# Row-wise dot products with a softmax: one transfer for the first x block, and the last store in two halves on two queues

## The chip, the cores and the metric

The kernel runs on one core of a Trainium2 chip. The metric is the device time of one execution in microseconds (us); before the change it is 320.69 us, the median of three runs (320.68 to 320.96).

## What is computed

```python
B, N, D = 8, 4096, 512          # x, y: float32, B x N x D
gram = np.matmul(x, y.transpose(0, 2, 1))
diag = np.diagonal(gram, axis1=1, axis2=2)
exp = np.exp(diag - diag.max(axis=-1, keepdims=True))
out = exp / exp.sum(axis=-1, keepdims=True)
```

Only the diagonal of the product is used. So the kernel needs, for each of the 8 x 4096 pairs of rows, the dot product of x's row with y's row (512 elements each), and then a softmax over the 4096 results of each batch. Both inputs are read once: 2 x 67.1 MB. The output is 8 x 4096 float32, 0.13 MB.

## The kernel before

**Tiling.** Four batches are worked on at a time (s = 0 and 1). A batch's 4096 rows lie over 32 partitions (G = 32), 128 rows to a partition, so four batches fill 128 partitions. A partition's 128 rows are taken in blocks of R = 32 rows, which makes S = 8 passes, t = 0 to 7: passes 0 to 3 are the first four batches, 4 to 7 the other four. A block is 64 KB in each partition, contiguous in memory, and 8 MB in all for x and the same for y.

**Buffers.** There are two tiles for x (xs, used in turn by t % 2) and a single one for y (ys), and a small tile, side, for the last K = 6 rows of y. The dot products go to diag[s], the softmax to res[s].

**Passes 0 to 5** (L118 to L131). x and y are loaded (load_x L63, load_y L66, both on the SyncE queue, SP). ScalarE copies y's last 6 rows to side (L123). VectorE multiplies the first 26 rows with y in place in xs (products, L70), which frees ys for the next load, then the last 6 with side, and adds up 30 rows (sums, L73). ScalarE adds up the other 2 (sums_act, L78). In pass 0, x comes in two transfers: rows 0 and 1, then rows 2 to 31 (L119 to L121). No instruction uses the first 2 rows alone: the first product reads rows 0 to 25.

**Pass 6** (L133 to L139) loads y in two halves. **Pass 7** (L141 to L150) loads x and y in pieces of 16, 8, 4, 2, 1 and 1 rows (x in pieces of at least 2), each followed by VectorE instructions that multiply and add up one row at a time (dots, L83).

**The end.** The softmax of the first four batches is stored by four transfers of 32 partitions each on SP (L155, L156). They are issued during pass 7. For the second four, exps takes the maximum (L97, L91) and exponentials with their sum (ScalarE, L104), normalize the total, its reciprocal and the product (L91, L110, L111), and ScalarE's queue (ACT) stores res[1], 128 partitions, in one transfer (L158). After it stand only the waits and barriers that end the program (L184 in the profile).

**What sets the order.** The order on each engine is the order in which the lines stand here; nothing is moved by a scheduler. Waits between engines are semaphores that the framework places. Transfers take eight semaphores in turn, so a transfer also waits until the one eight places before it has landed. SP's instructions are almost only such waits and issues: x of pass t+2 waits for the sums of pass t (its tile must be free), y of pass t+1 waits for the products of pass t.

Of the kernel before, what the change touches and what calls it, by code (L numbers as in the profile page):

```python
# [1 line left out]

# [5 lines left out]


@with_exitstack
def kernel(
    ctx: ExitStack,
    tc: tile.TileContext,
    x: bass.AP,
    y: bass.AP,
    out: bass.AP,
):
    nc = tc.nc
    ctx.enter_context(tc.manual_schedule())  # L20
    f32 = mybir.dt.float32
    Alu = mybir.AluOpType
    Act = mybir.ActivationFunctionType
    X = mybir.AxisListType.X
    B, N, D = x.shape
    P = nc.NUM_PARTITIONS
    G = 32
    Q = P // G
    C = N // G
    R = 32  # L30
    H = R // 2
    K = 6
    W = 2
    S = B // Q * (C // R)


    xv = x.rearrange("(s b) (j c) d -> s (b j) c d", b=Q, j=G)
    yv = y.rearrange("(s b) (j c) d -> s (b j) c d", b=Q, j=G)
    ov = out.rearrange("(s b) (j c) -> s (b j) c", b=Q, j=G)

    big = ctx.enter_context(tc.tile_pool(name="big", bufs=1))
    small = ctx.enter_context(tc.tile_pool(name="small", bufs=1))


    xs = [big.tile([P, R, D], f32, name=f"xs{i}") for i in range(2)]
    ys = big.tile([P, R, D], f32, name="ys")
    side = big.tile([P, K, D], f32, name="side")

    diag = [small.tile([P, C + i], f32, name=f"diag{i}") for i in range(B // Q)]
    res = [small.tile([P, C], f32, name=f"res{i}") for i in range(B // Q)]  # L50

    def columns(t, r0, n):
        c0 = t % (C // R) * R + r0
        return slice(c0, c0 + n)

    def rows(t, r0, n):
        return xs[t % 2][:, r0 : r0 + n, :]

    def dots_of(t, r0, n):
        return diag[t * R // C][:, columns(t, r0, n)]  # L60

    def load_x(t, r0, n):
        nc.sync.dma_start(out=rows(t, r0, n), in_=xv[t * R // C, :, columns(t, r0, n), :])  # L63

    def load_y(t, r0, n):
        nc.sync.dma_start(out=ys[:, r0 : r0 + n, :], in_=yv[t * R // C, :, columns(t, r0, n), :])  # L66

    def products(t, r0, n, yt):
        xt = rows(t, r0, n)
        nc.vector.tensor_tensor(out=xt, in0=xt, in1=yt, op=Alu.mult)  # L70

    def sums(t, r0, n):
        nc.vector.tensor_reduce(out=dots_of(t, r0, n), in_=rows(t, r0, n), axis=X, op=Alu.add)  # L73

    def sums_act(t, r0, n):
        for r in range(r0, r0 + n):
            row = xs[t % 2][:, r, :]
            nc.scalar.activation(out=row, in_=row, func=Act.Copy, accum_out=dots_of(t, r, 1))  # L78

    def dots(t, r0, n):  # L80
        for r in range(r0, r0 + n):
            xt = xs[t % 2][:, r, :]
            nc.vector.scalar_tensor_tensor(  # L83
                out=xt, in0=xt, scalar=1.0, in1=ys[:, r, :], op0=Alu.mult, op1=Alu.mult,
                accum_out=dots_of(t, r, 1),
            )

    def over_quadrant(name, column, op, negate=False):

        got = small.tile([P, 1], f32, name=name)  # L90
        nc.vector.tensor_reduce(  # L91
            out=got, in_=column.to_broadcast([P, G]), axis=X, op=op, negate=negate, apply_transpose=True
        )
        return got

    def largest(out, d):
        nc.vector.tensor_reduce(out=out, in_=d, axis=X, op=Alu.max)  # L97

    def exps(i, d):
        mxp = small.tile([P, 1], f32, name=f"mxp{i}")  # L100
        largest(mxp, d)
        nmx = over_quadrant(f"nmx{i}", mxp, Alu.max, negate=True)
        sump = small.tile([P, 1], f32, name=f"sump{i}")
        nc.scalar.activation(out=res[i], in_=diag[i][:, :C], func=Act.Exp, bias=nmx, scale=1.0, accum_out=sump)  # L104
        return sump

    def normalize(i, sump):
        total = over_quadrant(f"sum{i}", sump, Alu.add)
        rc = small.tile([P, 1], f32, name=f"rc{i}")
        nc.vector.reciprocal(out=rc, in_=total)  # L110
        nc.vector.tensor_single_scalar(out=res[i], in_=res[i], scalar=rc, op=Alu.mult)  # L111

    nc.vector.addr_align(128, offset=0, max_nops=0)
    nc.scalar.addr_align(128, offset=0, max_nops=0)

    for t in range(S - 2):  # L118
        if t == 0:  # L119
            load_x(t, 0, 2)  # L120
        load_x(t, 2 if t == 0 else 0, R - 2 if t == 0 else R)  # L121
        load_y(t, 0, R)
        nc.scalar.activation(out=side, in_=ys[:, R - K :, :], func=Act.Copy)  # L123
        if t == C // R:
            normalize(0, sump)
        products(t, 0, R - K, ys[:, : R - K, :])
        products(t, R - K, K, side)
        sums(t, 0, R - W)
        sums_act(t, R - W, W)
        if t == C // R - 1:  # L130
            sump = exps(0, diag[0])  # L131

    t = S - 2  # L133
    load_x(t, 0, R)
    for r0 in (0, H):
        load_y(t, r0, H)
        products(t, r0, H, ys[:, r0 : r0 + H, :])
    sums(t, R - H // 2, H // 2)
    sums_act(t, 0, R - H // 2)  # L139

    t += 1  # L141
    r0 = 0
    for n in (16, 8, 4, 2, 1, 1):
        if r0 < R - 1:
            load_x(t, r0, max(n, 2))
        load_y(t, r0, n)
        if r0 == R - 2:
            largest(diag[1][:, C:], diag[1][:, : C - 2])
        dots(t, r0, n)
        r0 += n  # L150

    met = small.tile([P, C - R], f32, name="met")
    nc.scalar.activation(out=met, in_=diag[1][:, : C - R], func=Act.Copy)  # L153

    for p, n in ((0, G), (G, G), (2 * G, G), (3 * G, G)):  # L155
        nc.sync.dma_start(out=ov[0, p : p + n, :], in_=res[0][p : p + n, :])  # L156
    normalize(1, exps(1, diag[1][:, C - 2 :]))
    nc.scalar.dma_start(out=ov[1], in_=res[1])  # L158


# [1 line left out]
_INS = ['x', 'y']  # L162
_OUTS = [((8, 4096), 'float32')]


# [23 lines left out]
```

## Time and profile before

| | us |
|---|---|
| median of three runs | 320.69 |
| span of the profiled execution | 318.87 |
| between the two | 1.82 |
| VectorE (DVE) busy | 244.7 (77%) |
| ScalarE (ACT) busy | 42.0 (13%) |
| bytes read / written | 134.22 MB / 0.13 MB |
| mean rate over the span | 421 GB/s |
| DMA queue of SP, share of the 16 DMA engines | 97.8% |
| DMA queue of ACT, share of the 16 DMA engines | 0.1% |

The span runs from the first to the last instruction of the profiled execution; the time of a run also holds what lies around it. All times in the text are counted from the span's start. A transfer is cut into packets, one for each partition here, that 16 DMA engines work through, 8 partitions to an engine. Each engine reports when its part has landed, so a transfer has 16 landing records, and the last of them ends the wait for it. The GB/s of a stretch count a packet where it starts; in a short stretch in which many long packets start the figure goes above the rate of the bytes.

### The profile page before, as it was taken

The numbers are of one execution on the slowest core, as the hardware profiler recorded it, in microseconds if no ns is written. First come the engines' busy times: TensorE is split into PE (matmuls) and PEld (weight loads), VectorE is DVE, ScalarE is ACT, GpSimd is POOL, SyncE is SP. The second block draws the span as 40 slices with busy tenths as digits, with TensorE's granted clock in tenths as the row PEclk, the third lists the DMA queues.
The fourth block names the chain that finished last, engine by engine and source line by source line (L and its number), as shares of the span: only waits on it lengthen the run. The fifth ranks groups of instructions, "written<-read, shape, count | busy, mean of one in ns | idle before, by whom it ended". The sixth has DMA issues, their size and how long they took to land.

```text
span 318.9 us, 304 instructions
## 1 busy us (share of the span) xinstructions
DVE 244.7 (77%) x96; ACT 42.0 (13%) x84; POOL 0.2 (0%) x4
## 2 busy tenths in 40 slices
DVE  0000069995899939999399994999949999996995
ACT  1000030100301003010120103000030100197000
POOL 0000000000000000000000000000000000000000
DMA  8989999999999999999999999999999899999993
GB/s 314 493 378 485 436 395 436 485 395 403 510 403 395 477 444 395 427 493 395 403 510 403 395 460 460 395 419 493 403 395 510 358 444 415 444 423 419 421 413 116
DMA packets 4226, 134.37 MB, mean 421 GB/s; under 512 B 512, under 2 KB 768, under 8 KB 1536
## 3 DMA queue, kind: packets, MB, share of 16 engines
q1 hardware_dynamic: 4080, 134.29, 97.8%
q10 hardware_dynamic: 144, 0.07, 0.1%
q14 instruction: 2, 0.02, 0.0%
HBM read 134.22 MB, written 0.13 MB: 421 GB/s over the span
## 4 chain that ended last, share of the span: by engine, by line
DMA 62%; DVE 35%; issue 2%; SPq 0%; ACT 0%; DVEq 0%
DMA ys<-in_y_dram 62%; DVE xs L70 30%; DVE diag L73 4%; DVE xs L83 0%; SPq L63 0%; DVE res L111 0%; DVE nmx L91 0%; DVE sum L91 0%; ACT res L104 0%; DVE rc L110 0%; DVE mxp L97 0%; DVEq L70 0%; SPq L66 0%; DVEq L83 0%
## 5 line engine op out<-in xcount | busy, mean ns | idle before, releaser
L70 DVE TENSOR_TENSOR xs<-xs,ys 128x13312 f32<-128x13312 f32 (+1 forms) x8 | 101.4, 12690 | 66.5 <-DMA ys<-in_y_dram 66.5
L73 DVE TENSOR_REDUCE diag<-xs 128x30 f32<-128x15360 f32 (+1 forms) x7 | 101.3, 14477 | 0.2
L78 ACT ACTIVATE xs<-xs 128x512 f32<-128x512 f32 x36 | 22.2, 616 | 111.0 <-DVE xs L70 111.0
L123 ACT ACTIVATE side<-ys 128x3072 f32<-128x3072 f32 x6 | 16.6, 2764 | 124.0 <-DMA ys<-in_y_dram 124.0
L83 DVE SCALAR_TENSOR_TENSOR xs<-xs,ys 128x512 f32<-128x512 f32 x32 | 19.9, 686 | 3.3 <-DMA ys<-in_y_dram 3.3
L70 DVE TENSOR_TENSOR xs<-xs,side 128x3072 f32<-128x3072 f32 x6 | 20.1, 3351 | 0.0
L78 ACT ACTIVATION_READ_ACCUMULATOR xs<-xs 128x1 f32 x36 | 6.7, 186 | 0.0
L104 ACT ACTIVATE res<-diag,nmx 128x128 f32<-128x128 f32 x2 | 0.8, 402 | 37.6 <-DVE nmx L91 37.6
L83 DVE DVE_READ_ACCUMULATOR xs<-xs,ys 128x1 f32 x32 | 2.6, 81 | 0.0
L123 ACT ACT_TABLE_LOAD x1 | 1.3, 1283 | 1.2 <-PEq L173 1.2
L91 DVE TRANSPOSE_TENSOR_REDUCE sum<-sump 128x1 f32<-128x32 f32 x2 | 0.4, 212 | 1.2 <-ACT res L104 1.2
L111 DVE TENSOR_SCALAR res<-res,rc 128x128 f32<-128x128 f32 x2 | 0.6, 286 | 0.1
L97 DVE TENSOR_REDUCE mxp<-diag 128x1 f32<-128x128 f32 (+1 forms) x2 | 0.4, 220 | 0.1
L91 DVE TRANSPOSE_TENSOR_REDUCE nmx<-mxp 128x1 f32<-128x32 f32 x2 | 0.4, 212 | 0.1
L110 DVE RECIPROCAL rc<-sum 128x1 f32<-128x1 f32 x2 | 0.3, 164 | 0.1
L104 ACT ACTIVATION_READ_ACCUMULATOR res<-diag,nmx 128x1 f32 x2 | 0.4, 186 | 0.0
L97 DVE TENSOR_REDUCE diag<-diag 128x1 f32<-128x126 f32 x1 | 0.3, 284 | 0.1
L153 ACT ACTIVATE met<-diag 128x96 f32<-128x96 f32 x1 | 0.3, 282 | 0.0
L173 POOL MEMSET const-bfloat16-1.0<- 128x1 bf16 x1 | 0.1, 102 | 0.0
L173 POOL MEMSET const-uint8-127<- 128x1 uint8 x1 | 0.1, 102 | 0.0
L173 POOL MEMSET const-float32-0.0<- 128x1 f32 x1 | 0.1, 99 | 0.2 <-issue 0.2
L173 POOL MEMSET const-float32-1.0<- 128x1 f32 x1 | 0.1, 99 | 0.0
## 6 DMA issues: line engine op xcount, KB each, us to landing
ys<-in_y_dram SPq DMA_DIRECT2D x3, 4096.0 KB, 16.0
xs<-in_x_dram SPq DMA_DIRECT2D x1, 7680.0 KB, 21.8
xs<-in_x_dram SPq DMA_DIRECT2D x1, 4096.0 KB, 14.9
xs<-in_x_dram SPq DMA_DIRECT2D x1, 2048.0 KB, 20.5
ys<-in_y_dram SPq DMA_DIRECT2D x1, 2048.0 KB, 17.2
xs<-in_x_dram SPq DMA_DIRECT2D x3, 512.0 KB, 22.1
xs<-in_x_dram SPq DMA_DIRECT2D x1, 1024.0 KB, 19.3
ys<-in_y_dram SPq DMA_DIRECT2D x1, 1024.0 KB, 21.3
```

The costliest lines, as they stand in the source:

```text
L70: nc.vector.tensor_tensor(out=xt, in0=xt, in1=yt, op=Alu.mult)
L73: nc.vector.tensor_reduce(out=dots_of(t, r0, n), in_=rows(t, r0, n), axis=X, op=Alu.add)
L78: nc.scalar.activation(out=row, in_=row, func=Act.Copy, accum_out=dots_of(t, r, 1))
L83: nc.vector.scalar_tensor_tensor(out=xt, in0=xt, scalar=1.0, in1=ys[:, r, :], op0=Alu.mult, op1=Alu.mult, accum_out=dots_of(t, r, 1),)
L91: nc.vector.tensor_reduce(out=got, in_=column.to_broadcast([P, G]), axis=X, op=op, negate=negate, apply_transpose=True)
L97: nc.vector.tensor_reduce(out=out, in_=d, axis=X, op=Alu.max)
L104: nc.scalar.activation(out=res[i], in_=diag[i][:, :C], func=Act.Exp, bias=nmx, scale=1.0, accum_out=sump)
L110: nc.vector.reciprocal(out=rc, in_=total)
L111: nc.vector.tensor_single_scalar(out=res[i], in_=res[i], scalar=rc, op=Alu.mult)
L123: nc.scalar.activation(out=side, in_=ys[:, R - K :, :], func=Act.Copy)
L153: nc.scalar.activation(out=met, in_=diag[1][:, : C - R], func=Act.Copy)
L173: nc = _bacc.Bacc("TRN2", target_bir_lowering=False, num_devices=1)
```

## The change

In pass 0, x is loaded in one transfer of 32 rows, as in the other passes. The last store is issued as two transfers: partitions 0 to 63 on SP, partitions 64 to 127 on ACT.

```diff
     for t in range(S - 2):
-        if t == 0:
-            load_x(t, 0, 2)
-        load_x(t, 2 if t == 0 else 0, R - 2 if t == 0 else R)
+        load_x(t, 0, R)
         load_y(t, 0, R)
...
     normalize(1, exps(1, diag[1][:, C - 2 :]))
-    nc.scalar.dma_start(out=ov[1], in_=res[1])
+    nc.sync.dma_start(out=ov[1, : 2 * G, :], in_=res[1][: 2 * G, :])
+    nc.scalar.dma_start(out=ov[1, 2 * G :, :], in_=res[1][2 * G :, :])
```

Instructions of VectorE, ScalarE and GpSimd stay as they are and in the same order. SP issues one load less at the start, and one store of 64 partitions more after the four stores of L156.

## The prediction

> **What bounds the kernel now.** I read the table of stretches first, one row for each pass of the loop over t. Its columns are the stretch and its length, busy us and instructions of DVE, ACT and POOL, the granted TensorE clock, the mean share of the 16 DMA engines, GB/s.
>
> ```profile
> 1.50:42.50 41.00, 0.04 (x1) 1.08 (x2) 0.00 (x0) 1.00 1.02 435
> 42.50:81.10 38.60, 33.41 (x3) 3.95 (x5) 0.00 (x0) 1.00 1.00 435
> 81.10:119.80 38.70, 33.45 (x3) 4.10 (x5) 0.00 (x0) 1.00 1.00 434
> 235.90:274.70 38.80, 38.74 (x4) 4.10 (x5) 0.00 (x0) 1.00 0.98 423
> 294.10:313.40 19.30, 18.90 (x61) 0.00 (x0) 0.00 (x0) 1.00 0.99 408
> 313.40:318.90 5.50, 2.34 (x9) 0.49 (x2) 0.00 (x0) 1.00 0.04 13
> ```
>
> The DMA engines are full from the first bytes to 313.4; VectorE has 5 us to spare in a pass. The next view, the chain that ended last in order of time, seems to say "DMA, then VectorE, then DMA", but its VectorE pieces are covered: while VectorE multiplies, x of the next pass streams in. The landing records of the trace (16 for each transfer, one from each DMA engine) settle it. From the last engine's landing of one 8 MB transfer to that of the next there are 19.34 to 19.36 us, from x of pass 1 to x of pass 6, without a longer step; the 4 MB ones take 9.71. So all that lies behind the first transfers hangs on one point: when the slowest DMA engine reaches steady flow. Move that by d, and all moves by d down to the last load (313.94), the 2.4 us of VectorE and ScalarE behind it, and the last store.
>
> **The first step's x.** The chain's beginning, and (second fence) the issues of the first 5 us with their size and time to landing:
>
> ```profile
> 0.73 0.40 SPq L63
> 1.13 0.06 issue
> 1.18 0.42 SPq L63
> 1.60 0.05 issue
> 1.65 40.68 DMA ys<-in_y_dram
> ```
>
> ```profile
> xs<-in_x_dram SPq DMA_DIRECT2D x1, 7680.0 KB, 21.8
> xs<-in_x_dram SPq DMA_DIRECT2D x1, 512.0 KB, 4.1
> ys<-in_y_dram SPq DMA_DIRECT2D x1, 40.7
> ```
>
> The 2 rows (512 KB) land 4.1 us after their issue, at 4.84; the 30 rows at 22.99, y at 42.33. 30 rows therefore cost 18.15 us in steady flow and 32 rows 19.35: **2 rows inside a long transfer cost 1.20**. Two rows as a transfer of their own cost 1.28 near the end (landing to landing, the 2-row x at 310.09 to 311.37 and 311.37 to 312.66). At the start they cost more. Stretches of half a microsecond:
>
> ```profile
> 0.00:1.75 1.75, 0.00 (x0) 0.59 (x1) 0.20 (x4) 1.00 0.00 0
> 1.75:2.25 0.50, 0.00 (x0) 0.50 (x1) 0.00 (x0) 1.00 0.98 229
> 2.25:2.75 0.50, 0.00 (x0) 0.19 (x1) 0.00 (x0) 1.00 0.67 221
> 2.75:3.25 0.50, 0.00 (x0) 0.00 (x0) 0.00 (x0) 1.00 1.14 344
> ```
>
> Until 3.25 the engines deliver 221 to 344 GB/s, against 435. The packet records tell how: the transfer is 128 packets of 4 KB, 8 for each engine. The first starts at 1.756; they last 234 ns in the mean and up to 655, where the 4 KB packets near the end last 163 ns. The first 60 KB packet of the 30 rows starts at 3.55 on the quickest engine, at 3.97 in the mean, at 4.44 on the slowest. From 1.756 that is 1.80 and 2.69 us for 8 packets that cost 1.28 when all runs: 0.5 us lost on the quickest engine, up to 1.4 on the slowest (less its own later start, which the records, without engine names, don't give). The spread of 0.9 us then stays to the end of the run.
>
> After the change the first transfer is 128 packets of 64 KB (the pieces the other full transfers have), and y's issue moves up by one slot of 0.45 us, behind 19 us of x: nothing comes of that. What the slowest engine saves is (4.44 minus its new starting point) minus 1.20. From both sides:
>
> - Least: all that was lost at the start is lost again. Saved are 1.28 - 1.20 = 0.08.
> - Most: it starts at 1.756 and loses nothing: 4.44 - 1.76 - 1.20 = 1.48.
>
> What decides is whether a slow first access hides behind a long packet. The nearest row is y of pass 0: a tensor not touched before, in 64 KB packets, and its 128 packets last 2.42 us in the mean, 2.51 at most, with no delay in its landings. A wait of some 0.3 us for a row's first bytes is seen when the packet ahead lasts 0.16 us, not when it lasts 2.42. So I take 7 of 8 such waits as hidden. Two things stay: the wait of each engine's first packet, 0.1 to 0.4 us by the packets above their 0.16 (165 to 524 ns among the first), and two packets of 8 KB of instructions that start at 1.77 and 2.89 and cost 2 x 0.31 = 0.62 us of some engine, probably the slowest. With them it starts at 1.76 + 0.62 + (0.1 to 0.5) = 2.5 to 2.9, so 4.44 - 1.20 - 2.5 to 2.9 = 0.3 to 0.75 saved. I take **-0.5**.
>
> The cover could go elsewhere: the instruction packets may now wait behind 64 KB packets, 2.4 us each. ScalarE first needs its table at 42.36 and VectorE works from 42.46, so this costs nothing.
>
> **The last store.** Timeline, the page's line on the issue, then two stretches:
>
> ```profile
> 316.16 0.29 DVE L111 TENSOR_SCALAR res<-res,rc 128x128 f32<-128x128 f32 x1
> 316.48 0.38 ACTq L158 DMA_DIRECT2D out_dram<-res  x1
> ```
>
> ```profile
> out_dram<-res ACTq DMA_DIRECT2D x1, 64.0 KB, 1.6
> ```
>
> ```profile
> 317.25:317.50 0.25, 0.00 (x0) 0.00 (x0) 0.00 (x0) 1.00 0.45 133
> 317.50:317.75 0.25, 0.00 (x0) 0.00 (x0) 0.00 (x0) 1.00 0.46 129
> ```
>
> VectorE ends at 316.45, ACT issues at 316.48, the first packet starts at 317.35, the last at 317.70, the landings come from 317.88 to 318.05; SP sees the last, and 0.8 us of closing steps end the span at 318.87. Of the 1.57 us from issue to last landing only the 0.35 between first and last packet can depend on how the rows are divided; the two stretches hold all of it, with the engines half busy.
>
> Removed: half of ACT's rows. Added: one issue on SP for the other half, with a wait for L111's result and one for an older load, landed by 313.94 and so free. SP issues a transfer of 32 rows in 0.31 to 0.36 (L156) and one of 128 in 0.33 when it has been idle: rows don't set the price, and the two issues lie side by side. SP has been free since 310.42. Behind its wait stand only the closing waits, four of which passed at 314.13 to 314.70; passed later they take some 0.3 us after 316.85 and are over by 317.2, ahead of the landing. SP wakes 0.07 after VectorE (56.50 to 56.57), ACT 0.03: 0.04 late.
>
> Each engine still moves 8 packets of 27 ns (0.22 us) and now two semaphore packets of 9. If handing out descriptors sets the 0.35, two queues bring it to the engines' 0.23: -0.12. If both issues pass through one place in turn, the second half starts an issue slot later, as SP's own back-to-back issues do (287.02 to 287.50): +0.47, and one more closing wait is +0.07 (318.07 to 318.13). Between -0.12 and +0.54 the rows near it (half-busy engines, 0.04 late) stand close to nothing: I take **0.0**.
>
> The Trainium skill has a rule against this edit. "DMA: Bandwidth & Descriptors", section "Rules for kernel authors", says of two transfers to disjoint halves of the partitions not to bother, because both halves go through the same 16 engines. By it the halves save nothing, the sum stays -0.5; were each half a stream of its own at half the 0.35, it would be -0.7. No row of this trace has a transfer in two halves on two queues.
>
> **Sum.** 318.87 - 0.5 + 0.0 = 318.37. The median lies 1.82 above the span (320.69); taken as unchanged, that gives **320.2 us**.
>
> **Rivals.**
>
> 1. *The start stays as slow.* The losses are paid per row of x, not per short packet: only 0.08 goes. For it: the long packets fall among the later ones of the eight too, not only the first. Against it: y's 2.51 at most. 320.6.
> 2. *The start is nearly clean.* The instruction packets are on another engine than the slowest, or slip in unseen: -0.9 to -1.48. For it: steady flow loses nothing anywhere else. 319.2 to 319.8, say 319.6.
> 3. *The second half of the store comes late.* +0.54 against -0.5: 320.7, no change. For it: nothing but that no row shows two queues at the end; against it: ACT and SP have a queue each in the table of queues.
> 4. *Slower: the short rows were an opener.* The place is x's first 128 packets. The 60 KB packets all last 2.267 us, on rows that the 2-row transfer touched just before. If a first touch costs a 64 KB packet what the worst 4 KB ones show, 655 - 163 = 0.5 us, on all 8 packets, this is +4.0 against the up to 1.4 now lost there: +2.6, 323.3. It decides from 0.19 us a packet (1.48/8), packets of 2.61 us. Against it: y's packets, first touches too, with 2.42.
>
> That the edits don't do what they say is excluded by the compiled order: SP has one load less and one store of 64 rows more, ACT's store has 64 rows; nothing else moves.
>
> **Chances.** Forecast (-0.2 to -0.85) 0.53; rival 1 0.18; rival 2 0.14; rival 3 0.09; rival 4 0.06. Two tenths of a percent, 0.64 us, is about what a measurement of this kernel can tell from no change: faster means under 320.05. That holds rival 2 and a third of the forecast's case: 0.32. Slower, over 321.33, is rival 4 alone (rivals 1 and 3 together would give 321.15): 0.06. The rest, 0.62, is within. The range of 8 in 10 takes in rivals 1 and 3, the forecast's case and the near half of rival 2: 319.5 to 320.85.
>
> **What would show it.** Right: x of pass 0 lands about 0.5 us before 22.99, its first packets last near 2.42 us, and every later landing down to the last is early by the same amount; from the end of L111 to the span's end stays 2.4. Rival 1: x lands within 0.1 of 22.99. Rival 4: packets of over 2.6 us at the start. Rival 3: the landings of the two halves lie apart by some 0.4. The forecast is wrong if a later landing step differs from 19.35, which would mean that the spread of the engines matters.

## The result, and the profile after

The changed kernel takes 321.22 us (median of 18 runs, 321.18 to 321.64), the kernel before 320.69 (18 runs, 320.51 to 321.47): a ratio of 1.0015, 95% interval 1.0009 to 1.0021. It is half a microsecond slower where 0.5 us less was forecast, outside the range of 319.5 to 320.85. The spans of the two profiled executions are 318.87 before and 319.51 after.

The table of stretches of the changed kernel, with the same columns as before:

```profile
1.50:42.50 41.00, 0.00 (x0) 0.97 (x2) 0.00 (x0) 1.00 1.02 435
81.10:119.80 38.70, 33.45 (x3) 4.10 (x5) 0.00 (x0) 1.00 1.00 434
294.10:313.40 19.30, 18.97 (x61) 0.00 (x0) 0.00 (x0) 1.00 0.98 404
313.40:319.50 6.10, 2.35 (x9) 0.49 (x2) 0.00 (x0) 1.00 0.05 12
```

What bounds the kernel has not changed: the DMA engines are full to 313.4. The new time is in the last row, which reaches to the end of the span: 6.1 us instead of 5.5 with the same instructions of VectorE and ScalarE in it. The landing records agree: every pass from the first x on takes 19.34 to 19.36 us on the last engine, as before. So the two edits can be read apart, one at each end of the run.

**The start.** The chain's first pieces in the changed kernel, and three stretches of it:

```profile
0.73 0.40 SPq L63
1.13 0.06 issue
1.19 41.26 DMA ys<-in_y_dram
```

```profile
1.75:2.25 0.50, 0.00 (x0) 0.50 (x1) 0.00 (x0) 1.00 5.02 1720
2.25:2.75 0.50, 0.00 (x0) 0.19 (x1) 0.00 (x0) 1.00 1.04 393
2.75:3.25 0.50, 0.00 (x0) 0.00 (x0) 0.00 (x0) 1.00 0.00 0
```

y is issued 0.46 earlier and lands at 42.45 instead of 42.33. The stretches can't be compared with those of before: all 16 first packets, 64 KB each, are counted where they start, between 1.77 and 2.58. Their lengths say more: 2.53 to 3.32 us, 2.98 in the mean, where the later ones last 2.42. The first x lands at 23.10 on the last engine, 22.74 on the one before it and 22.24 in the median; before it was 22.99, 22.68 and 22.47. Between these two profiles the median engine gained 0.23 and the last one lost 0.11, and the last one sets every wait. The gain of the median is not the edit's: in the six other profiles below that keep the 2 rows ahead and start as early (e2, e3, e4, e8, e12, e15) the median engine lands at 22.02 to 22.09 and the last one at 22.80 to 23.03; with one transfer (the changed kernel, e1, e5, e6, e7) it is 22.14 to 22.26 and 22.96 to 23.10. So the profile of before was late on its median engine, and with one transfer both come a little later in the mean. The last load that VectorE waits for lands at 313.44 (313.31), and L111 ends at 316.51 (316.45): half of the loss is won back on the way, as told below.

**The end.** Timeline of the changed kernel, then the page's lines on the two issues:

```profile
316.23 0.28 DVE L111 TENSOR_SCALAR res<-res,rc 128x128 f32<-128x128 f32 x1
316.54 0.53 SPq L156 DMA_DIRECT2D out_dram<-res  x1
316.55 0.55 ACTq L157 DMA_DIRECT2D out_dram<-res  x1
```

```profile
out_dram<-res SPq DMA_DIRECT2D x1, 32.0 KB, 1.8
out_dram<-res ACTq DMA_DIRECT2D x1, 32.0 KB, 2.1
```

The two issues lie side by side, as forecast, but each takes 0.53 to 0.55 where the whole store took 0.38, and the halves land 1.8 and 2.1 us after their issue where the whole took 1.6. In the stretches one sees the packets come later and over a longer time than before:

```profile
317.50:317.75 0.25, 0.00 (x0) 0.00 (x0) 0.00 (x0) 1.00 0.07 16
317.75:318.00 0.25, 0.00 (x0) 0.00 (x0) 0.00 (x0) 1.00 0.55 123
318.00:318.25 0.25, 0.00 (x0) 0.00 (x0) 0.00 (x0) 1.00 0.54 121
```

SP's 64 packets start from 317.71 to 317.98, ACT's from 317.98 to 318.26: one half after the other. From the end of L111 to the span's end there are 2.995 us instead of 2.418, +0.58: 0.30 more from issue to first packet (1.17 against 0.88), 0.22 more from there to the last landing (0.92 against 0.70), 0.06 more from the last landing to the span's end (0.875 against 0.813). The 0.06 is not the second store's. SP closes with waits for the eight semaphores in a fixed order. Before, the wait for ACT's store is the last one, at 318.07; in the changed kernel, with one load less, its semaphore is the last but one, passed at 318.65, and one more wait passes at 318.71. e1 below, with one load less and the whole store, has 0.877; e2, with the two halves and all loads, has 0.813.

### The profile page after: what moved, and what is told of

The parts are those of the page before. It is cut to its first block, busy times and chain, and to the rows that moved or that the text cites. A ratio compares the mean times of both kernels' runs of the same rounds, so it can differ in the third digit from the quotient of the medians.

```text
span 319.5 us, 304 instructions
## 1 busy us (share of the span) xinstructions
DVE 244.8 (77%) x96; ACT 42.0 (13%) x84; POOL 0.2 (0%) x4
## 4 chain that ended last, share of the span: by engine, by line
DMA 62%; DVE 35%; issue 2%; SPq 0%; ACT 0%; DVEq 0%
DMA ys<-in_y_dram 62%; DVE xs L70 30%; DVE diag L73 4%; DVE xs L83 0%; SPq L63 0%; DVE res L111 0%; DVE nmx L91 0%; DVE sum L91 0%; ACT res L104 0%; DVE rc L110 0%; DVE mxp L97 0%; DVEq L70 0%; SPq L66 0%
## 5 line engine op out<-in xcount | busy, mean ns | idle before, releaser
L83 DVE SCALAR_TENSOR_TENSOR xs<-xs,ys 128x512 f32<-128x512 f32 x32 | 20.0, 686 | 3.2 <-DMA ys<-in_y_dram 3.2
L83 DVE DVE_READ_ACCUMULATOR xs<-xs,ys 128x1 f32 x32 | 2.6, 81 | 0.0
L111 DVE TENSOR_SCALAR res<-res,rc 128x128 f32<-128x128 f32 x2 | 0.6, 286 | 0.1
```

What stands on the lines that cost most here:

```text
L83: nc.vector.scalar_tensor_tensor(out=xt, in0=xt, scalar=1.0, in1=ys[:, r, :], op0=Alu.mult, op1=Alu.mult, accum_out=dots_of(t, r, 1),)
```

## The experiments

My theory after the result: the two edits add up, the store costs about 0.58 and the first load gains nothing. (The 0.58 turned out to be 0.52 of the store and 0.06 of the order of the closing waits.) Timed runs stand beside runs of the kernel before on the same chip.

**The edits apart.** e1_x_only makes the first edit alone:

```diff
-        if t == 0:
-            load_x(t, 0, 2)
-        load_x(t, 2 if t == 0 else 0, R - 2 if t == 0 else R)
+        load_x(t, 0, R)
```

> The first x in one transfer, the last store whole on ACT as before. Theory (the two edits add up; the changed kernel lost 0.58 us behind L111 by the store and 0.07 ahead of it by the first load): span near 318.93, 320.6 to 320.8, no change within 0.2%; the slowest engine's first x lands near 23.1, not 0.5 us before 22.99. Rival (the store costs little, and the first load costs the half microsecond in runs other than the profiled one): 321.1 or more. The forecast on record for this edit: -0.5, 320.2.

Measured: 320.69 (320.60 to 320.95, 11 runs) beside 320.80; ratio 0.9995 (0.9986 to 1.0003). No difference; the first x lands at 22.97. The theory holds, the rival and the forecast's -0.5 fall; by the interval at most 0.45 us can have been saved.

e2_store_only makes the second alone:

```diff
-    nc.scalar.dma_start(out=ov[1], in_=res[1])
+    nc.sync.dma_start(out=ov[1, 0:64, :], in_=res[1][0:64, :])
+    nc.scalar.dma_start(out=ov[1, 64:128, :], in_=res[1][64:128, :])
```

> The first x in 2 and 30 rows as before, the last store as halves on SP and ACT. Theory: the time from the end of L111 to the span's end is 3.0 instead of 2.42, so 321.2 to 321.3, 0.55 us above before. Rival (the delay of the halves comes from elsewhere, such as the rotation of the transfer semaphores, which is shifted by one place against the changed kernel): 320.7.

Measured: 321.18 beside 320.80; ratio 1.0012 (1.0003 to 1.0020), +0.38. In its profile L111's end stands 2.94 ahead of the span's end (2.42 before), +0.52. The store is the loss, with the semaphores in another rotation too. The two medians, -0.11 and +0.38, add up to less than the +0.53 of the whole change, but each has some 0.27 of uncertainty either way; the lowest times do add up (+0.15 and +0.54 against +0.67).

**Why two halves are slow.** e3_halves_on_sp issues both from SP, e4_whole_on_sp the whole store from SP.

```diff
-    nc.scalar.dma_start(out=ov[1], in_=res[1])
+    nc.sync.dma_start(out=ov[1, 0:64, :], in_=res[1][0:64, :])
+    nc.sync.dma_start(out=ov[1, 64:128, :], in_=res[1][64:128, :])
```

> The first x as before; the last store as two halves of 64 partitions, both issued by SP, one after the other. Theory A (a second issue costs one issue slot whichever queue carries it, since both queues' issues pass one place in turn): the second half's first packet starts some 0.3 to 0.47 after the first's, 0.4 to 0.6 us above before, like the halves on two queues. Theory B (two queues that issue at once slow each other down, one queue alone doesn't): each issue keeps 0.33 to 0.43, the first half's packets start 0.88 after its issue, and the loss is 0.2 to 0.3 us.

```diff
-    nc.scalar.dma_start(out=ov[1], in_=res[1])
+    nc.sync.dma_start(out=ov[1], in_=res[1])
```

> The first x as before; the last store whole, on SP instead of ACT. Theory (the number of issues is what costs, not the queue): first packet 0.88 after the issue, packets over 0.35, landing 1.6 after the issue; 320.65 to 320.8, no change. Rival (SP's queue is the slow one, because it has carried 134 MB or because its closing waits now stand behind the issue): 0.2 us or more above before.

Timelines of e3 (two lines) and e4:

```profile
316.35 0.53 SPq L158 DMA_DIRECT2D out_dram<-res  x1
316.92 0.59 SPq L159 DMA_DIRECT2D out_dram<-res  x1
```

```profile
316.47 0.35 SPq L158 DMA_DIRECT2D out_dram<-res  x1
```

e3: 321.54 beside 320.80, ratio 1.0025 (1.0016 to 1.0035), +0.74; in its profile the second half's packets start 0.64 after the first's, more than theory A had. e4: 320.65, ratio 1.0000 (0.9991 to 1.0008), its first packet 0.85 after the issue. So the queue doesn't matter for a whole store. What neither theory of e3 had said: **the first issue of 64 partitions takes 0.53 with nothing beside it**, and its first packet comes 1.17 after it. Two queues at once don't slow each other's issue; something in the half itself does. e8_64_alone tests that:

```diff
-    nc.scalar.dma_start(out=ov[1], in_=res[1])
+    nc.scalar.dma_start(out=ov[1, 0:64, :], in_=res[1][0:64, :])
```

> The first x as before; of the last store only partitions 0 to 63 are stored, by ACT alone; the other half is left out. Theory G (a store of 64 partitions is slow in itself: 0.53 of issue and 1.17 to the first packet, where one of 128 takes 0.38 and 0.88): the same 0.53 to 0.55 and 1.15 to 1.2 here, landing 1.8 to 1.85 after the issue, so a half stored alone ends later than the whole. Rival (the second issue is what slows): 0.38, 0.88, landing at 1.5 after the issue.

Its timeline, and the line on its issue:

```profile
316.61 0.54 ACTq L158 DMA_DIRECT2D out_dram<-res  x1
```

```profile
out_dram<-res ACTq DMA_DIRECT2D x1, 32.0 KB, 1.8
```

One half, alone, lands later than the whole (1.84 against 1.57 after the issue), and its 64 packets last 34 ns in the mean, where the 128 of the whole lasted 27. From L111's end to the span's end it is 2.69, +0.27: this is about half of the store's 0.52. The rest comes where two halves are stored: the second half's packets start 0.27 behind the first's (0.28 in e2). e15_64_mid asks for the place of the half (partitions 32 to 95):

> As e8_64_alone, but the one half that is stored is partitions 32 to 95 (the rest is left out). If the price of a 64-partition store is the count: issue 0.53 to 0.55, landing 1.8 to 1.85 after it, as for partitions 0 to 63. If it is where the half begins and ends: other than that.

```profile
316.59 0.60 ACTq L158 DMA_DIRECT2D out_dram<-res  x1
```

Issue 0.60, landing 1.86 after it, a little above what was expected of the count alone, so the place may add 0.06 to the issue. It doesn't help; the count is what the two share, though the packets last 27 ns again. e12_sp32_act96 divides the store differently:

```diff
-    nc.scalar.dma_start(out=ov[1], in_=res[1])
+    nc.sync.dma_start(out=ov[1, 0:32, :], in_=res[1][0:32, :])
+    nc.scalar.dma_start(out=ov[1, 32:128, :], in_=res[1][32:128, :])
```

> The first x as before; the last store as 32 partitions on SP and 96 on ACT. Theory G (a transfer of 64 partitions is slow in itself, one of 32 is not: 0.31 to 0.36 in L156): SP's issue 0.33, its first packets 0.9 after it; what 96 cost on ACT no run shows, between 0.38 and 0.55, so the second landing comes 1.6 to 2.1 after the issue, +0.1 to +0.55 us. Rival (any two issues come in turn, 0.27 apart, whatever their shape): the same +0.55 as with 64 and 64.

```profile
316.36 0.32 SPq L158 DMA_DIRECT2D out_dram<-res  x1
316.37 0.39 ACTq L159 DMA_DIRECT2D out_dram<-res  x1
```

```profile
out_dram<-res ACTq DMA_DIRECT2D x1, 48.0 KB, 1.6
out_dram<-res SPq DMA_DIRECT2D x1, 16.0 KB, 1.5
```

320.88 beside 320.75, ratio 1.0001 (0.9992 to 1.0011): no difference. The issues take 0.32 and 0.39, first packets come at 317.18 and 317.26, hardly one after the other, and from L111's end to the span's end it is 2.47, 0.06 more than before: ACT's 96 land 1.63 after their issue where the whole took 1.57, and the closing steps take the 0.81 of before. Theory G stands, the rival (any two issues come 0.27 apart) falls. Two queues cost next to nothing here; 64 partitions do. Why a transfer of 64 is slower to issue than one of 32, 96 or 128, no run here shows.

**Why the start gained nothing.** First what else goes on in those microseconds. e5_late_issues moves the issues of the first y and the second x out of them, e6_late_issues_table the table load too:

```diff
+    nc.vector.memset(ys[:, :H, :], 0.0)
+    nc.vector.memset(xs[1][:, :1, :], 0.0)
+    late = small.tile([P, 8], f32, name="late")              # e6 alone
+    nc.vector.memset(late, 0.0)                              # e6 alone
+    nc.scalar.dma_start(out=late, in_=xv[0, :, 0, :8])       # e6 alone
     for t in range(S - 2):
```

> The first x in one transfer and the last store whole on ACT (as in e1_x_only); VectorE first writes zeros into half of ys and one row of the second x tile, so that the issues of the first y and of the second x wait some 5 us behind it; x streams until 21, so that nothing waits for them. Theory I (the first packets last 2.9 to 3.2 us instead of 2.42 because SP hands out two more transfers of 128 packets in that time): they last near 2.42, the first x lands at 22.3 or earlier, 0.5 us under e1_x_only. Theory S (the wait belongs to the first packet of each engine, whatever else goes on): they last 2.9 to 3.2 again, the first x lands at 22.9 to 23.1, no change.

> As e5_late_issues, and a 4 KB load on ACT's queue that waits for the same zeros stands ahead of ScalarE's table load, so that the table is loaded some 5 us later than at 1.16. Theory T (the table load and its instruction packets slow the first packets): first packets near 2.42 and the first x at 22.3 or earlier here, and not in e5. Theory S: 2.9 to 3.2 in both.

Measured: 320.73 and 320.74 beside 320.79, ratios 0.9998 (0.9989 to 1.0007) and 0.9997 (0.9988 to 1.0006). First packets 2.97 in the mean in both, the first x at 23.03 and 23.04. (The zeros took longer than I had reckoned; y was issued at 9.97.) Theory I falls, and T for the table load, which e6 makes at 10.95; the two fetches of instructions stay in e6, at 1.95 and 4.76, and e9 below starts without them. S stands. e7_short_programs shortens the programs of ScalarE and VectorE: it leaves out most of the row sums, whose results stay zero.

```diff
-        for r in range(r0, r0 + n):
-            row = xs[t % 2][:, r, :]
-            nc.scalar.activation(out=row, in_=row, func=Act.Copy, accum_out=dots_of(t, r, 1))
+        row = xs[t % 2][:, r0, :]
+        nc.scalar.activation(out=row, in_=row, func=Act.Copy, accum_out=dots_of(t, r0, 1))
...
-        for r in range(r0, r0 + n):
+        for r in range(r0, r0 + 1):
             xt = xs[t % 2][:, r, :]
...
+    for d in diag:
+        nc.gpsimd.memset(d, 0.0)
```

> The first x in one transfer, the last store whole; left out: of every group of rows that ScalarE adds up, and of every group of pass 7, all but the first (their results stay zero), so that ScalarE has some 33 activations fewer and VectorE 26 products fewer. Theory F (the last engine of the first x is the one that fetches 8 KB of instructions a second time between its 64 KB packets, 0.3 to 0.4 us, and whose next packet then lasts 0.45 to 0.55 us longer): without the second fetch the last engine lands within 0.15 of the one before it, at 22.8 or earlier. Rival (the fetch belongs to something else than the length of the programs): two fetches of 8 KB again, and an engine 0.15 to 0.35 behind the rest.

Both fetches are there again, and the last engine lands 0.29 behind the next (23.03 and 22.74). Programs of this length are still fetched in two pieces, so this run did not take the fetch away, and theory F was not put to the test by it. But the trace of each merged kernel (the changed one, e1, e5, e6, e7) shows the same thing on one engine: 8 KB of instructions between the first and the second 64 KB packet, 0.31 us (0.41 in e1), and the packet that starts as the fetch ends lasts 2.95 us (2.87 in e1) instead of 2.42. That engine is 0.85 us behind its own flow, and its second packet ends last of all 16 in each of the five, 0.03 to 0.23 behind the next. The first fetch, at 1.76 to 2.02, goes to another engine: in each of the five a first packet starts just as it ends, on an engine that is not the last. With 2 rows ahead the second fetch comes at 2.58 to 2.97, among 4 KB packets.

Then the first packets themselves. e9_late_start issues the first x when all is quiet, e10_warm_x and e11_warm_y load 32 bytes of every row of x or of y long before, e13_late_pitch reads rows 66 KB apart:

```diff
+    warm = small.tile([P, 8], f32, name="warm")              # e10 and e11 alone; e11: yv
+    nc.sync.dma_start(out=warm, in_=xv[0, :, 0, :8])
+    nc.vector.memset(xs[0][:, :H, :], 0.0)
     for t in range(S - 2):
```

> The first x in one transfer, last store whole; VectorE first writes zeros into half of the first x tile, so that the first load is issued near 9.97 instead of 0.73 (the run is some 9 us longer for it). Theory P (the long first packet is the wait of an engine's first read, whenever it comes): the 16 first packets last 2.9 to 3.2 again. Theory C (the chip's first microseconds are slow, until some 3.3): they last 2.42 to 2.5, and both instruction fetches are over before.

> As e9_late_start, and a load of 32 bytes of each of the 128 rows of x (128 packets of 32 bytes) is issued at 0.73. Theory R (what costs is the first touch of each row's memory): first packets of x near 2.42 here, where e9 has 2.9. Theory C: 2.42 in both; if the queue's first use is what costs, 2.42 here and also in e11_warm_y.

> As e10_warm_x, but the 32 bytes come from the 128 rows of y. Theory R: first packets of x as in e9 (2.9), not as in e10. Theory Q (the first use of the queue or of the engines): 2.42 as in e10.

> As e9_late_start (first x in one transfer, issued near 9.97, after all else is quiet), but the 128 rows of the first x are read from places 66 KB apart instead of 256 KB (other data, so pass 0 computes other products). Theory B (a transfer that starts from rest pays once, on each engine's first packet, some 0.4 to 0.7 us until bytes flow): the 16 first packets last 2.8 to 3.2 as in e9. Theory L (16 engines that start in step on rows a power of two apart get in each other's way until they have spread out): 2.42 to 2.6, and the landings of the first x lie closer together than the 0.79 of e9.

The means of the 16 first packets are 2.99 (e9), 2.98 (e10), 3.05 (e11) and 2.97 (e13). Not the chip's first microseconds, not the first touch of rows, not the queue's first use, not the distance of the rows: theories C, R, Q and L fall. (e10 touched only 32 bytes of each 64 KB; but every later load of the kernel is a first touch too, and its packets last 2.42.) What is common to all is a transfer that starts on engines at rest, and the same +0.54 stands on the one packet behind a fetch. Theory B (paid once, where the flow starts) is what is left; it is argued, not shown. In its words "on each engine's first packet" it does not hold: of the first packets, the five that start 0.97 to 1.38 behind the first of the 16 (two in e1, one each in e6, e7 and e13) last 2.42 to 2.49, nearly as in flow. The excess stands on those that start earlier, and what makes it no run here shows. e14_late_split puts the 2 rows ahead again, at the same late time:

> As e9_late_start, but the first x in 2 and 30 rows. Theory B (the start is paid once, by the 2 rows or by the 32, and two rows apart cost only 1.28 - 1.20 = 0.08 more): the last landing of the 30 rows comes 22.0 to 22.2 after the first issue, against 21.99 in e9. The forecast's reason (eight waits, one for each short packet): 22.4 or more.

Timelines of e9 and of e14: the first VectorE instruction of pass 0, which waits for y; then e14's issues of x.

```profile
51.41 14.02 DVE L70 TENSOR_TENSOR xs<-xs,ys 128x13312 f32<-128x13312 f32 x1 [41.47 <-DMA ys<-in_y_dram]
```

```profile
51.15 14.03 DVE L70 TENSOR_TENSOR xs<-xs,ys 128x13312 f32<-128x13312 f32 x1 [41.21 <-DMA ys<-in_y_dram]
```

```profile
xs<-in_x_dram SPq DMA_DIRECT2D x1, 7680.0 KB, 21.2
xs<-in_x_dram SPq DMA_DIRECT2D x1, 512.0 KB, 3.4
```

Both first loads are issued at 9.97. On the median engine all of x has landed 21.36 us later in one transfer and 21.45 in two: 0.09, less than the 0.20 by which the four late runs with one transfer differ there (21.32 to 21.52). On the last engine it is 21.99 against 21.69, 0.30 lost, below what I expected of theory B: after the short packets the 16 engines lie closer together (0.38 between first and last landing, 0.79 in e9). The forecast's reason, eight waits for eight packets, falls. That the last engine is earlier with two transfers rests, for a quiet start, on e14 alone, and the merged runs differ among themselves (e10 has 21.79, e11 22.03). In time it brought nothing (330.06 and 329.65, one run each): some of e14's later passes are longer, as told at the end.

## Why the prediction was wrong, point by point

- **What bounds the kernel**: right. The DMA engines are full from the first bytes to the last load, and a shift at the start goes through to the end: +0.11 at the first x, +0.13 at the last load.
- **The first load, -0.5 forecast, +0.11 measured** at x, and -0.1 to 0 in time (e1). Two steps failed. "So I take 7 of 8 such waits as hidden": what the runs point to is not eight waits but one start, which the eight short packets paid in pieces and the one long packet pays whole (argued from e9 to e14; what a start costs an engine stays open). The long ones last 0.46 to 0.63 more than in flow, in the mean of each run. For the short ones I estimate 0.41 to 0.51 (from the mean start of the first sixteen 4 KB packets to that of the first sixteen 60 KB ones, less the 1.28 of the flow), and 0.81 in the profile of before, the one that the forecast was read from. The row that I took as nearest, y of pass 0, was a first touch of memory, but not a start from rest, since x was flowing ahead of it. And "the wait of each engine's first packet, 0.1 to 0.4 us": with 0.56 in the mean, 0.11 to 0.90 by engine, it was too small; the packet behind the second fetch, another 0.54, was not in the sum. The first fetch, reckoned at 0.31 on the same engine, lasts 0.46 to 0.93 in the five merged kernels (1.06 before), but on an engine that is not the last. Whether the lower bound, 0.08 saved, is right can't be told from these runs.
- **"The cover could go elsewhere"**: the instruction packets did come to stand behind 64 KB packets (the second at 4.85 instead of 2.89). ScalarE lost nothing by it, as forecast. The cost came back the other way, on the loads behind it.
- **The last store, 0.0 forecast, +0.58 measured**, 0.52 of it the store's (e2). The step that failed is "rows don't set the price": from 0.31 to 0.36 for 32 rows and 0.33 for 128 I concluded on 64, which no row showed, and 64 take 0.53 to 0.55 and hold the first packet back by 0.30. Of the rest, "If both issues pass through one place in turn" gives the picture of two halves of 64, whose packets start 0.27 apart, but it is no rule for any two issues: 32 and 96 start 0.08 apart. "One more closing wait" did not come with the second store: the closing steps of e2 and e12 take the 0.81 of before. That the upper bound, +0.54, is nearly the price is luck: it is made of a whole issue slot (0.47) and that wait (0.07), and the slowness of a half by itself, 0.27 in e8, is not in it.
- **The Trainium skill's rule** against two halves of the partitions ("DMA: Bandwidth & Descriptors", section "Rules for kernel authors") was right in its advice. Its reason, the 16 engines that both share, says that nothing is gained; it names no cost. Here 64 and 64 cost 0.52, and 32 and 96 next to nothing (0.06).
- **A term that was not in the sum**: the order of waits. One load less moves the rotation of the eight semaphores by one. The row before the last (L83) waits for x and for y; before, the wait for y, which comes last, stood as an instruction of its own ahead of it, and 0.09 passed from landing to start (313.31 to 313.40); now the wait for x stands there, long over, and 0.02 pass (313.44 to 313.46). That won back 0.07, and the same rotation lost 0.06 again in the closing waits.
- **Chances and range.** Rivals 1 and 3 together are 321.15 in the prediction, and the measured time is 321.22. I had priced each against the forecast's value for the other, so the range ended below their sum. They lie at two ends of the run and don't exclude each other. Both came true in number rather than in reason. Rival 1 has x within 0.1 of 22.99, and it is 0.11 behind; but the losses are not paid per row of x, since the 112 packets after the first 16 last 2.42 in the mean. Rival 3's late second half is there, 0.27 behind instead of 0.4. Rival 4's sign, packets over 2.6 at the start, was there on the first 16 alone, and not the +2.6 us that 128 of them would have cost.

## What to carry to other kernels

When a bound is set by two rows, of 32 and of 128, the case between them is not covered: look whether the very shape is in the trace, and keep the upper bound in the range if it isn't. In these runs the first transfer paid about half a microsecond at its start whether it was cut or not, so cutting or merging it moved little. One profile can be untypical in just the place that a forecast is read from, as the start of the one before was. Edits at different ends of a run add up, also where both go wrong, and the range has to hold that sum.

## What the runs showed that I had not expected

- A store of 64 partitions of 512 bytes, alone, takes longer from issue to landing (1.84 to 1.9 us) than one of 128 (1.57), with an issue of 0.54 to 0.60 against 0.38; 32 and 96 side by side take 1.5 and 1.6.
- A fetch of 8 KB of instructions between two 64 KB packets of an engine costs it 0.31 us, and then the next packet 0.54 more (0.41 and 0.45 in e1).
- Passes are not always 19.35, and that seems to hang on the first load. Of the eight profiled executions with the 2 rows ahead (before, e2, e3, e4, e8, e12, e14, e15), five have passes of 19.37 to 19.74 us on the last engine, two to seven of the twelve, 0.09 to 0.8 us in all; in e2 four passes between 81 and 159 last 19.37, 19.55, 19.59 and 19.38. Of the nine with one transfer (the changed kernel, e1, e5 to e7, e9 to e11, e13) none has one over 19.365, but for 19.395 in the pass of e6 that holds its extra 4 KB load. The times point the same way: the 32 runs of before beside e1 reach from 320.45 to 321.27, the 11 of e1 from 320.60 to 320.95 (one of e6 has 321.35). So the merged load doesn't lower the fastest time, but seems to take away part of the scatter. In the five the engines' landings move closer together or apart during such passes (0.99 to 0.82 in e2); but closeness alone is not the reason, since e13 runs at 0.66 to 0.70 without one. The cause stays open.
